# Gated sigmoid (GLU): the loads from tile 2 on issued by GpSimd's software DMA queue

## The chip, the cores and the metric

One Trainium2 chip, one of its cores. The metric is device time in microseconds (us), the median over runs of the whole kernel. The core has five engines that matter here by these names: DVE (VectorE), ACT (ScalarE), POOL (GpSimd), PE (TensorE, not used) and SP (SyncE, which only issues DMAs). Each engine runs its own queue of instructions in order; engines wait for each other by semaphores. A DMA is issued by an engine's queue and carried out by 16 DMA engines, which move data between HBM (main memory) and SBUF (on-chip memory of 128 partitions).

## The reference

```python
def setup_inputs():
    return {
        "x": np.random.randn(8192, 8192).astype(np.float32),
    }

def reference(x: np.ndarray) -> np.ndarray:
    a, b = np.split(x, 2, axis=-1)
    return a * (1 / (1 + np.exp(-b)))
```

The left half of each row is multiplied by the sigmoid of the right half. 268.4 MB are read and 134.2 MB are written, all fp32.

## The kernel before

The 8192 rows are cut into 32 tiles of 256 rows. A tile puts two neighbouring rows of x on each of the 128 partitions (`R = 2`), so each partition's part of a load is one run of 64 KB in HBM and in SBUF, and of a store one run of 32 KB. A tile's load is 8.39 MB, its store 4.19 MB. There are two input buffers (`xs`, called x_sb in the profile) and two output buffers (`os`, called o_sb); tile i uses number i % 2 of each (`SLOTS = 2`).

The loop over tiles (lines 93 to 103) does three things for tile i:

- `work` (line 72): ACT computes the sigmoid of the right half in place (line 82), then a multiply writes the output buffer (line 84). A middle tile is worked in two pieces: columns 0 to 768 of both halves' 4096 (`cut`, the shape 128x1536 with two rows to a partition), whose multiply runs on POOL from tile 2 on, and the rest (128x6656), whose multiply runs on DVE. Tile 0 and tile 31 are worked in four pieces of 128x2048, with all multiplies on DVE.
- `load(i + 2)` (line 59): the load into the input buffer that tile i has just been read from. It waits for the multiplies of tile i, on POOL and on DVE. It is issued on SP's queue (line 63). Loads 0 and 1 are issued ahead of the loop, load 0 in two halves.
- `store(i)` (line 66): issued on ACT's queue (line 68) after the multiplies of tile i. Tile 0 stores in halves as its pieces are done, tile 31 in a half and two quarters.

In the middle tiles, ACT's sigmoid waits for the tile's load and also for the store of tile i - 2, which frees the output buffer (line 81); the multiplies then need no wait of their own for it.

The order on each queue is the program's order (`place`, line 48), and waits that follow from others are dropped there. `_launch_early` (line 106) puts the first load, on SP, ahead of the entry's barrier. `_close_on_sync` (line 119) rewrites the end: POOL waits for all semaphores but the last store's and clears them, and SP waits for the last store.

Of the kernel before, what the change touches and what calls it, by code (L numbers as in the profile page):

```python
# [8 lines left out]
def _tiles(ctx, tc, x, out):  # L9
    nc = tc.nc  # L10
    P = nc.NUM_PARTITIONS
    DEP = mybir.DependencyInfo(mybir.DependencyClass.Sync, mybir.DependencyReason.DATA)
    fp32 = mybir.dt.float32
    SIG = mybir.ActivationFunctionType.Sigmoid

    n_rows, n_cols = x.shape
    half = n_cols // 2
    R = 2
    SLOTS = 2
    n_tiles = n_rows // (P * R)  # L20
    x_g = x.rearrange("(g p h r) m -> g h p (r m)", p=P, h=2, r=R)
    out_g = out.rearrange("(g p h r) m -> g h p (r m)", p=P, h=2, r=R)

    pool = ctx.enter_context(tc.tile_pool(name="io", bufs=1))
    xs = [pool.tile([P, R * n_cols], fp32, name=f"x_sb{k}") for k in range(SLOTS)]
    os = [pool.tile([P, R * half], fp32, name=f"o_sb{k}") for k in range(SLOTS)]

    whole = [(0, 8)]
    rows = [(0, 4), (4, 8)]
    cut = half // 16 * 3  # L30
    few_and_most = [(0, 8, 0, cut), (0, 8, cut, half)]
    fourths = [(k, k + 2, k % 4 * half // 4, (k % 4 + 2) * half // 4) for k in range(0, 8, 2)]
    loads = [whole] * n_tiles
    works = [few_and_most] * n_tiles
    stores = [whole] * n_tiles
    behind = [0] * n_tiles
    loads[0] = stores[0] = rows
    works[0] = works[-1] = fourths
    stores[-1] = [(0, 4), (4, 6), (6, 8)]
    behind[-1] = 1  # L40

    def meet(a, b):
        return a[0] < b[1] and b[0] < a[1]

    traced = [[] for _ in range(SLOTS)]
    load_of, mul_of, store_of = {}, {}, {}

    def place(i, ins, *needs):


        kept = {n.ins.name for n in needs}
        for e in traced[i % SLOTS]:
            if e.ins.name not in kept:
                tc.declare_no_dep(ins.ins, e.ins, reason="follows from the waits that are kept")
        traced[i % SLOTS].append(ins)
        tc.keep_in_program_order(ins)
        return ins

    def load(i):
        for lo, hi in loads[i]:  # L60
            c = slice(lo * n_cols // 4, hi * n_cols // 4)
            free = [m for w, m in mul_of.get(i - SLOTS, []) if meet(w, (lo, hi))]
            ins = nc.sync.dma_start(out=xs[i % SLOTS][:, c], in_=x_g[i // 2, i % 2, :, c])  # L63
            load_of.setdefault(i, []).append(((lo, hi), place(i, ins, *free)))

    def store(i, lo, hi):
        c = slice(lo * half // 4, hi * half // 4)
        ins = nc.scalar.dma_start(out=out_g[i // 2, i % 2, :, c], in_=os[i % SLOTS][:, c])  # L68
        done = [m for w, m in mul_of[i] if meet(w, (lo, hi))]
        store_of.setdefault(i, []).append(((lo, hi), place(i, ins, *done)))  # L70

    def work(i, lo, hi, near, far):

        rows = xs[i % SLOTS].rearrange("p (r h m) -> p r h m", r=R, h=2)
        packed = os[i % SLOTS].rearrange("p (r m) -> p r m", r=R)
        r, c = slice(lo // 4, (hi + 3) // 4), slice(near, far)
        b = rows[:, r, 1, c]
        landed = [s for w, s in load_of[i] if meet(w, (lo, hi))]
        gone = [s for w, s in store_of.get(i - SLOTS, []) if meet(w, (lo, hi))]
        by_sigmoid = 0 < i < n_tiles - 1  # L80
        needs = [*landed, *(gone if by_sigmoid else ())]
        sig = place(i, nc.scalar.activation(out=b, in_=b, func=SIG), *needs)  # L82
        engine = nc.gpsimd if far == cut and i > 1 else nc.vector
        mul = engine.tensor_mul(out=packed[:, r, c], in0=rows[:, r, 0, c], in1=b)  # L84
        if by_sigmoid:
            for s in gone:
                tc.add_manual_dep(sig.ins, s.ins.name, DEP, reason="frees the output slot")
        place(i, mul, sig, *(() if by_sigmoid else gone))
        mul_of.setdefault(i, []).append(((lo, hi), mul))

    for i in range(SLOTS):
        load(i)
    for i in range(n_tiles):
        due = list(stores[i])
        for k, piece in enumerate(works[i]):
            work(i, *piece)
            ready = works[i][k - behind[i]][1] if k >= behind[i] else 0
            while len(stores[i]) > 1 and k < len(works[i]) - 1 and due[0][1] <= ready:
                store(i, *due.pop(0))
        if i + SLOTS < n_tiles:  # L100
            load(i + SLOTS)
        for lo, hi in due:
            store(i, lo, hi)
# [115 lines left out]
```

## Time and profile before

| | |
|---|---|
| Median of 3 runs | 932.47 us (932.45 to 932.73) |
| The profiled execution's own time | 932.5 us |
| Its span, first to last instruction | 931.1 us |
| DVE busy, idle before its instructions | 232.5 us, 690.2 us, all for ACT |
| ACT busy, longest wait | 229.8 us, 630.0 us in 29 waits for stores |
| POOL busy, idle | 99.9 us, 787.7 us, for ACT |
| Loads on SP's queue (q1) | 33 DMAs, 4,752 packets, 268.44 MB |
| Stores on ACT's queue (q10) | 35 DMAs, 5,040 packets, 134.22 MB |
| Issue to landing, median | load 43.5 us, store 43.6 us |

How to read the profile: the span is cut into 40 equal slices, and one digit gives the busy share of a slice in tenths (9 is 90% or more); DMA is the mean over the 16 DMA engines. A queue row gives packets, MB and the share of 16 engines' span that its packets took. A timeline row gives the start and the length in us, the engine and line, the operation with out<-in, the count, and in brackets how long the engine sat idle before and for whom; "SPq" and "ACTq" are issues of DMAs, and where several instructions are merged in a row its length runs from the first to the last of them. The chain is the work that ended last, followed back from the end of the span. A row of the stretch table gives the stretch, its length, the busy time and the number of instructions of DVE, ACT and POOL, the TensorE clock, the DMA share and the GB/s moved. Small packets of under 512 B are those that end a DMA, 16 to each.

### The profile page before, as it was taken

The numbers are of one execution on the slowest core, as the hardware profiler recorded it, in microseconds if no ns is written. First come the engines' busy times: TensorE is split into PE (matmuls) and PEld (weight loads), VectorE is DVE, ScalarE is ACT, GpSimd is POOL, SyncE is SP. The second block draws the span as 40 slices with busy tenths as digits, with TensorE's granted clock in tenths as the row PEclk, the third lists the DMA queues.
The fourth block names the chain that finished last, engine by engine and source line by source line (L and its number), as shares of the span: only waits on it lengthen the run. The fifth ranks groups of instructions, "written<-read, shape, count | busy, mean of one in ns | idle before, by whom it ended". The sixth has DMA issues, their size and how long they took to land.

```text
span 931.1 us, 325 instructions
## 1 busy us (share of the span) xinstructions
DVE 232.5 (25%) x39; ACT 229.8 (25%) x69; POOL 99.9 (11%) x33
## 2 busy tenths in 40 slices
DVE  1133311333113331133320333203332033320233
ACT  2123332033320333203332023320233302333023
POOL 0001111011110111101111011110111101111010
DMA  9999999999999999999999999999999999999998
GB/s 405 450 439 417 428 450 424 455 405 428 450 428 450 407 469 409 428 450 427 452 405 450 428 428 450 424 452 408 428 450 428 450 408 465 411 428 450 427 452 383
DMA packets 9793, 402.67 MB, mean 432 GB/s; under 512 B 1088, under 2 KB 1088, under 8 KB 1088
## 3 DMA queue, kind: packets, MB, share of 16 engines
q1 hardware_dynamic: 4752, 268.44, 66.6%
q10 hardware_dynamic: 5040, 134.22, 33.4%
q14 instruction: 1, 0.01, 0.0%
HBM read 268.44 MB, written 134.22 MB: 432 GB/s over the span
## 4 chain that ended last, share of the span: by engine, by line
DMA 75%; DVE 12%; ACT 12%; issue 0%; ACTq 0%; SPq 0%
DMA out_dram<-o_sb 65%; DVE o_sb L84 12%; ACT x_sb L82 12%; DMA x_sb<-in_x_dram 10%; ACTq L68 0%; SPq L63 0%
## 5 line engine op out<-in xcount | busy, mean ns | idle before, releaser
L84 DVE TENSOR_TENSOR o_sb<-x_sb 128x6656 f32<-128x6656 f32 (+2 forms) x39 | 232.5, 5970 | 690.2 <-ACT x_sb L82 690.2
L82 ACT ACTIVATE x_sb<-x_sb 128x1536 f32<-128x1536 f32 (+1 forms) x68 | 228.5, 3407 | 689.9 <-DMA out_dram<-o_sb 630.0
L84 POOL TENSOR_TENSOR o_sb<-x_sb 128x1536 f32<-128x1536 f32 x29 | 99.7, 3437 | 787.7 <-ACT x_sb L82 787.7
L82 ACT ACT_TABLE_LOAD x1 | 1.3, 1283 | 0.8 <-PEq L203 0.8
L203 POOL MEMSET const-float32-0.0<- 128x1 f32 x1 | 0.1, 98 | 0.2 <-issue 0.2
L203 POOL MEMSET const-bfloat16-1.0<- 128x1 bf16 x1 | 0.1, 101 | 0.0
L203 POOL MEMSET const-uint8-127<- 128x1 uint8 x1 | 0.1, 101 | 0.0
L203 POOL MEMSET const-float32-1.0<- 128x1 f32 x1 | 0.1, 98 | 0.0
## 6 DMA issues: line engine op xcount, KB each, us to landing
out_dram<-o_sb ACTq DMA_DIRECT2D x30, 4096.0 KB, 43.6
x_sb<-in_x_dram SPq DMA_DIRECT2D x2, 4096.0 KB, 16.4
out_dram<-o_sb ACTq DMA_DIRECT2D x3, 2048.0 KB, 28.0
out_dram<-o_sb ACTq DMA_DIRECT2D x2, 1024.0 KB, 8.3
x_sb<-in_x_dram SPq DMA_DIRECT2D x31, 43.5
```

What stands on the lines that cost most here:

```text
L82: sig = place(i, nc.scalar.activation(out=b, in_=b, func=SIG), *needs)
L84: mul = engine.tensor_mul(out=packed[:, r, c], in0=rows[:, r, 0, c], in1=b)
L203: nc = _bacc.Bacc("TRN2", target_bir_lowering=False, num_devices=1)
```

## The change

From tile 2 on, a load is issued by GpSimd instead of SP. Loads 0 (two halves) and 1 stay on SP. The buffers, the bytes, the access patterns, what a load waits for and the place of its issue in the program stay as they are, and the stores stay on ACT's queue.

```diff
@@ -60,7 +60,8 @@
         for lo, hi in loads[i]:
             c = slice(lo * n_cols // 4, hi * n_cols // 4)
             free = [m for w, m in mul_of.get(i - SLOTS, []) if meet(w, (lo, hi))]
-            ins = nc.sync.dma_start(out=xs[i % SLOTS][:, c], in_=x_g[i // 2, i % 2, :, c])
+            queue = nc.sync if i < SLOTS else nc.gpsimd
+            ins = queue.dma_start(out=xs[i % SLOTS][:, c], in_=x_g[i // 2, i % 2, :, c])
             load_of.setdefault(i, []).append(((lo, hi), place(i, ins, *free)))
```

## The prediction

> **What bounds the kernel now.** I read the page's summary, its queues and its chain first, then the DMA view and the timeline of two tiles in the middle, then the stretch table of the end.
>
> ```profile
> span 931.1 us, 325 instructions
> DVE 232.5 (25%) x39; ACT 229.8 (25%) x69; POOL 99.9 (11%) x33
> DMA  9999999999999999999999999999999999999998
> q1 hardware_dynamic: 4752, 268.44, 66.6%
> q10 hardware_dynamic: 5040, 134.22, 33.4%
> DMA 75%; DVE 12%; ACT 12%; issue 0%; ACTq 0%; SPq 0%
> x_sb<-in_x_dram SPq DMA_DIRECT2D x31, 43.5
> ```
>
> Every compute engine idles for three quarters of the span, and the DMA engines never do. The chain names DVE and ACT for 24%, but the row of DMA shares is 9 right through: while they work, the transfers of other tiles go on. So the time is bytes over rate, 402.67 MB at 432 GB/s.
>
> One stretch of two tiles, 506 to 564 us, in the DMA view and the stretch table:
>
> ```profile
> DMA packets 576, 25.17 MB, mean 434 GB/s; under 512 B 64, under 2 KB 64, under 8 KB 64
> q1 hardware_dynamic: 288, 16.78, 66.7%
> q10 hardware_dynamic: 288, 8.39, 33.5%
> 506.00:564.00 58.00, 14.18 (x2) 14.28 (x5) 6.87 (x2) 1.00 1.00 434
> ```
>
> 288 packets for two loads is 2 x (128 rows + 16 small ones); a row of a load is one packet of 64 KB, a row of a store one of 32 KB. A load packet takes 0.667 x 16 x 58 / 256 = 2.418 us of its engine, a store packet 0.335 x 16 x 58 / 256 = 1.214 us. Eight of each per tile and engine are 19.3 + 9.7 = 29.0 us, and a tile takes 29.0 us. Twice 1.214 less 2.418 leaves 0.010 us: the fixed cost of a packet.
>
> The timeline from 99 us shows the slack:
>
> ```profile
> 99.66 7.12 ACT L82 ACTIVATE x_sb<-x_sb 128x1536 f32<-128x1536 f32 x2 [21.82 <-DMA out_dram<-o_sb]
> 101.22 3.44 POOL L84 TENSOR_TENSOR o_sb<-x_sb 128x1536 f32<-128x1536 f32 x1 [25.51 <-ACT x_sb L82]
> 106.81 7.09 DVE L84 TENSOR_TENSOR o_sb<-x_sb 128x6656 f32<-128x6656 f32 x1 [21.85 <-ACT x_sb L82]
> 113.97 29.33 SPq L63 DMA_DIRECT2D x_sb<-in_x_dram  x2
> 113.99 0.35 ACTq L68 DMA_DIRECT2D out_dram<-o_sb  x1
> 128.66 7.12 ACT L82 ACTIVATE x_sb<-x_sb 128x1536 f32<-128x1536 f32 x2 [21.88 <-DMA out_dram<-o_sb]
> 130.22 3.44 POOL L84 TENSOR_TENSOR o_sb<-x_sb 128x1536 f32<-128x1536 f32 x1 [25.56 <-ACT x_sb L82]
> ```
>
> A tile is worked in 14.3 us (99.66 to 113.97), and then its x slot's next load and its store are issued together. That load lands 43.5 us later, of which its own packets, one for one with the stores, take 29.0. For the first 14.5 us it only queues behind the load before it.
>
> **The change, part by part.** Thirty of 33 load DMAs (4,320 of the 4,752 packets, 30 x 8.39 = 251.7 MB) leave SP for POOL.
>
> Removed: 30 issues of 0.33 us on SP, which runs nothing else and spends its time waiting. Worth 0.
>
> Moved, issue: the load waits for DVE's multiply at L84, now on POOL. Ahead of it there stands only POOL's own 3.44 us multiply of that tile, ended at 104.7, before DVE's at 113.9. Behind it stands POOL's multiply of the next tile at 130.22, which itself waits for ACT's work on a load that lands later. POOL is free for 130.2 - 114.0 = 16.2 us. Stores stay on ACT's queue and pass nothing. Worth 0.
>
> Added, making the descriptors by software: no row shows it. Below it is SP's 0.33 us; above, POOL's fixed work is seen only inside a 3.44 us multiply. I take the upper row. The cover is the 14.5 us of the load before, so either is hidden; the first one (tile 2, issued after 28 us) has load 1 in the queue until 46.3 us. Past 14.5 us the load is late, ACT's next sigmoid is late with it, and stores fill the engines for a while. Worth 0.
>
> A rule of the Trainium skill speaks against this part: SBUF — State Buffer, "SBUF: two separate sides", says that a GpSimd-issued DMA cannot write its descriptors while VectorE holds the port pair they share. In this trace DVE ends its multiply before the load is released and starts its next one 21.9 us later, so even a full lock would cost nothing; by rule and by row the sum is the same here unless generation lasts those 21.9 us.
>
> Moved, transfer: this is the only part on the path that sets the end. Each engine carries 30 x 8 = 240 of these packets, so each 10 ns more or less on a packet is 2.4 us. Low end: the whole fixed part vanishes, -2.4 us. High end: each 64 KB row is cut into sixteen 4 KB pieces, each paying 10 ns: 15 x 0.010 x 240 = +36 us. The access pattern and the bytes are unchanged, and the nearest row is the same row on the hardware queue, so I take 0 and keep -2.4 and +36.
>
> The end, which depends on the shares of the two queues:
>
> ```profile
> 897.20 0.34 ACTq L68 DMA_DIRECT2D out_dram<-o_sb  x1
> 911.66 5.51 ACT L82 ACTIVATE x_sb<-x_sb 128x2048 f32<-128x2048 f32 x3 [21.67 <-DMA x_sb<-in_x_dram]
> 918.13 0.34 ACTq L68 DMA_DIRECT2D out_dram<-o_sb  x1
> ```
>
> When load 31 lands at 911.7, store 30 (issued 897.2, behind store 29) still has its 9.7 us to go, until 921.4; the last tile's first store is issued at 918.1, so the engines stay full, and 9.7 us more end at 931.1, the span. One load packet for one store packet keeps this. Worth 0.
>
> Sum: span 931.1 + 0 = 931.1. The profiled run took 932.5, 1.4 more than its span, and the median is 932.47; what lies outside the span is kept. Forecast **932.5 us**. About 0.2% (1.9 us) is what a measurement of this kernel can tell from no change.
>
> **Rivals.**
>
> *Dearer or smaller packets (slower).* The software queue cuts rows, or its packets cost the engines more. It decides from 8 ns a packet (240 x 0.008 = 1.9 us). For it: the engines have no idle time to hide any of it. Against: nothing in the access pattern changes. With rows in halves, 32 KB against 32 KB, the fixed part costs 240 x 0.010 = 2.4 us, and stores get half of the engines: in the 14.5 us before load 31 lands, store 30 moves 7.2 of its 9.7 us, 2.5 are left, and the engines stand empty until the first store at 6.5 + 0.3 us: 4.3 us. Time 932.5 + 6.7 = 939. With 4 KB pieces, 36 + 6.8 = 43, time 975. Unequal engines belong here: one engine 1% slower on loads costs 1% of 30 x 19.3, 5.8 us, time 938. A sentence on the skill: DMA: Bandwidth & Descriptors, "Latency and other measured facts", says that engines 7 and 15 usually lag and suspects the software rings; it gives no size, and the present shares, all on hardware queues, cannot show it.
>
> *A load's whole share as one packet (slower).* If a queue is left only after all eight rows of an engine (19.3 us), loads push stores aside, both x slots fill, and ACT waits for the store that frees the output slot (29 times already, 630.0 us in the waits). Then two tiles take 14.3 of work, one store packet (1.2), a load (19.3), one store packet (1.2), a load (19.3) and the other six packets of the store that ACT waits for (7.3): 62.6 us instead of 58.0, because only one store (9.7 us) is there to cover 14.3 us of work. 15 pairs x 4.6 = 69, time 1,002. Against: today's queues change over after each row. The same page of the skill, "Queues, rings and completion order", calls 9 to 17 descriptors per packet typical; its section "SWDGE vs HWDGE vs iDMA" has packets of preferably 4096 B, which would leave a row by itself.
>
> *A late issue (slower).* Generation holds POOL longer than the 14.5 us of cover. At 20 us each slot's cycle of two tiles grows by at most 20 - 14.5 = 5.5 us (less where stores have drained meanwhile and the load runs alone), 15 x 5.5 = 83, time up to 1,015. Against: 44 times SP's issue would be needed.
>
> *Cheaper packets (faster).* The fixed 10 ns falls away on loads: 932.5 - 2.4 = 930.1. More is not to be had, since the bytes already move at 434 GB/s.
>
> That the change does nothing is excluded by its text; it would show as 4,752 packets on q1.
>
> **How the numbers follow.** Forecast 0.43 (931 to 934), dearer or smaller packets 0.30, whole share 0.10, late issue 0.07, cheaper 0.10. The predicted time is the forecast's. The range runs from 929.8 (just below the cheaper packets) to 955, which takes in the halves, the uneven engines and about a third of the way to the 4 KB pieces: 0.43 + 0.10 + some 0.25 + 0.02 is 0.80. Faster 0.10, same 0.43, slower 0.30 + 0.10 + 0.07 = 0.47.
>
> **What would show it.** Right: q1 keeps 432 packets, a new queue has 4,320 with a share near 62.4% (66.6 x 30 / 32); tiles 29.0 us apart; sigmoid starts unmoved against landings; POOL's multiply not later. Dearer packets: more of them or a larger share for the same bytes. Whole share: tiles in pairs, DMA slices below 9. Late issue: loads begin long after DVE ends. I am wrong if steady tiles move by over 0.06 us each, or the gap after the last load grows beyond 19.5 us.

## The result, and the profile after

The changed kernel takes 940.59 us (median of 4 runs, 940.3 to 940.8) against 932.5: a ratio of 1.0085, 95% interval 1.0073 to 1.0097. It is slower by 8.1 us, under 1% and well clear of the noise. The time lies inside the range, on the slower side; the forecast itself, no change, was wrong.

From the page of the changed kernel, its span, queues and chain, and the row of the issues on POOL:

```profile
span 939.4 us, 329 instructions
DMA  9998999999999999999999999999999999999998
q0 software_dynamic: 4320, 251.66, 61.9%
q10 hardware_dynamic: 5040, 134.22, 33.2%
q1 hardware_dynamic: 432, 16.78, 4.2%
DMA 70%; issue 12%; ACT 10%; DVE 4%; another core or an unknown queue 3%; ACTq 0%; POOLq 0%
L64 POOL DMA_DIRECT2D x_sb<-in_x_dram x30 | 17.8, 594 | 346.3 <-issue 215.7
```

The new queue q0 has the 4,320 packets that were to move, and they are no dearer: 0.619 (the 61.9%) x 16 x 939.4 us over 3,840 rows of data is 2.42 us, as before. An issue keeps POOL for 0.594 us. The only digit that differs in kind is the 8 in the fourth slice, 70 to 94 us. The middle is unchanged too; the stretch 506 to 564 us in the DMA view:

```profile
DMA packets 576, 25.17 MB, mean 434 GB/s; under 512 B 64, under 2 KB 64, under 8 KB 64
q0 software_dynamic: 288, 16.78, 66.7%
q10 hardware_dynamic: 288, 8.39, 33.5%
```

This is row for row what the kernel before has there, with q0 in the place of q1. The loss is at both ends. Rows of the timeline of the start, in the kernel before and then in the changed kernel:

```profile
46.29 7.12 ACT L82 ACTIVATE x_sb<-x_sb 128x1536 f32<-128x1536 f32 x2 [20.90 <-DMA x_sb<-in_x_dram]
70.71 7.12 ACT L82 ACTIVATE x_sb<-x_sb 128x1536 f32<-128x1536 f32 x2 [17.30 <-DMA out_dram<-o_sb]
```

```profile
28.44 0.71 POOL L64 DMA_DIRECT2D x_sb<-in_x_dram  x1 [28.00 <-DVE o_sb L85]
58.41 7.12 ACT L83 ACTIVATE x_sb<-x_sb 128x1536 f32<-128x1536 f32 x2 [33.01 <-DMA x_sb<-in_x_dram]
72.97 0.53 POOL L64 DMA_DIRECT2D x_sb<-in_x_dram  x1 [43.81 <-DVE o_sb L85]
73.16 7.12 ACT L83 ACTIVATE x_sb<-x_sb 128x1536 f32<-128x1536 f32 x2 [7.62 <-DVE o_sb L85]
108.50 7.12 ACT L83 ACTIVATE x_sb<-x_sb 128x1536 f32<-128x1536 f32 x2 [28.22 <-DMA x_sb<-in_x_dram]
```

Tile 1 starts at 58.41 us; it started at 46.29. Tile 2 starts at 73.16, straight after tile 1: its load was there already. The DMA view says why, first of the kernel before while it waits for load 1 (28.4 to 46.3 us), then of the changed kernel (28.5 to 58.4):

```profile
q1 hardware_dynamic: 112, 6.29, 81.2%
q10 hardware_dynamic: 112, 1.57, 20.5%
```

```profile
q0 software_dynamic: 96, 6.29, 48.7%
q1 hardware_dynamic: 96, 5.24, 41.2%
q10 hardware_dynamic: 112, 1.57, 12.3%
```

In the changed kernel load 1 (q1), load 2 (q0) and store 0 (q10) share the engines packet by packet: without the 16 small ones that end a DMA, the three queues have 80, 96 and 96 packets. On one queue load 2 stands behind load 1; on a queue of its own it stands beside it. By 58.4 us load 2 has 6.29 of its 8.39 MB, and load 1 is 12 us late. What follows, in the stretch table of the changed kernel (stretch, its length, busy time of DVE, ACT and POOL, TensorE clock, DMA share, GB/s):

```profile
28.40:58.40 30.00, 0.00 (x0) 0.00 (x0) 0.71 (x1) 1.00 1.02 437
69.50:73.50 4.00, 3.16 (x1) 0.34 (x1) 0.53 (x1) 1.00 0.10 41
926.00:929.00 3.00, 3.00 (x2) 1.66 (x2) 0.00 (x0) 1.00 0.16 66
```

While three queues share, the rate is full (437 GB/s), so the sharing itself loses nothing. But when load 1 lands, both input buffers are nearly full and little is left to move, the rest of load 2 and of store 0 (2.1 MB each). The next transfers are issued 14.3 us (a store) and 14.6 us (a load) later, when tile 1 has been worked, and the engines run dry: a share of 0.10 over 4 us, 3.6 us lost. The second hole is at the end, 3 us at 0.16, 2.5 us lost. The waits name its cause, before and after, and so do the stores' times from issue to landing, before and after:

```profile
ACT x_sb L82 <- DMA out_dram<-o_sb: 630.0, 29, 22.1
ACT x_sb L83 <- DMA x_sb<-in_x_dram: 690.8, 32, 33.0
out_dram<-o_sb ACTq DMA_DIRECT2D x30, 4096.0 KB, 43.6
out_dram<-o_sb ACTq DMA_DIRECT2D x30, 4096.0 KB, 32.7
```

Before, ACT waited 630.0 us in 29 waits for stores; now in 32 waits it is loads. A store used to land 43.6 us after its issue and now lands after 32.7. So the stores' arrears, by which they had been landing late since the first tiles, are gone: during the wait for load 1 and the dry stretch, stores caught up. So after load 31 lands, at 921.6, less is left of store 30 than the 9.7 us of before, and the engines empty before the last tile's first store at 928.08:

```profile
921.61 5.51 ACT L83 ACTIVATE x_sb<-x_sb 128x2048 f32<-128x2048 f32 x3 [21.81 <-DMA x_sb<-in_x_dram]
928.08 0.34 ACTq L69 DMA_DIRECT2D out_dram<-o_sb  x1
```

3.6 and 2.5 are 6.1 of the 8.1 us. The trace's record of each packet accounts for the other 2: packets that ran longer than they do in the middle (2.418 us for a row of a load, 1.213 for a row of a store) add up, per DMA engine, to 2.3 us more than before, 1.2 of it in loads and 1.1 in stores; most of it, 1.6, stands between 75 and 110 us, just after the first dry stretch. What made these packets longer was not found. In the middle the tiles' starts drift by 0.9 us in 26 tiles (tile 4 to tile 30, 755.07 against 754.20 us), 0.03 a tile. The account is complete without this, and packets that match it were not found.

### The profile page after: what moved, and what is told of

It reads as the page before. It is cut to its first block, busy times and chain, and to the rows that moved or that the text cites. A ratio compares the mean times of both kernels' runs of the same rounds, so it can differ in the third digit from the quotient of the medians.

```text
span 939.4 us, 329 instructions
## 1 busy us (share of the span) xinstructions
DVE 232.5 (25%) x39; ACT 229.8 (24%) x69; POOL 117.6 (13%) x63
## 3 DMA queue, kind: packets, MB, share of 16 engines
q0 software_dynamic: 4320, 251.66, 61.9%
## 4 chain that ended last, share of the span: by engine, by line
DMA 70%; issue 12%; ACT 10%; DVE 4%; another core or an unknown queue 3%; ACTq 0%; POOLq 0%
DMA x_sb<-in_x_dram 70%; ACT x_sb L83 10%; DVE o_sb L85 4%; ACTq L69 0%; POOLq L64 0%
## 5 line engine op out<-in xcount | busy, mean ns | idle before, releaser
L64 POOL DMA_DIRECT2D x_sb<-in_x_dram x30 | 17.8, 594 | 346.3 <-issue 215.7
## 6 DMA issues: line engine op xcount, KB each, us to landing
out_dram<-o_sb ACTq DMA_DIRECT2D x30, 4096.0 KB, 32.7
```

The lines of the kernel that those rows point to most:

```text
L64: ins = queue.dma_start(out=xs[i % SLOTS][:, c], in_=x_g[i // 2, i % 2, :, c])
```

## The experiments

The theory, called "handover" in the expectations: nothing about the software queue costs time; it is that two neighbouring loads stand on two queues, once, at a moment when one store is all the other work there is. The rivals: a one-off cost when the software queue is first used, and dearer packets on it. Landings and packets that stand in no row shown here are from the traces' records of each packet. Each kernel was timed beside the kernel before on the same chip, and ratios are to it.

**Keeping the two loads apart.**

```diff
+            if i == SLOTS:
+                for _, s in load_of[i - 1]:
+                    tc.add_manual_dep(ins.ins, s.ins.name, DEP, reason="the load before has landed")
```

> Load 2, the first on POOL, also waits until load 1 has landed. Handover (two loads on two queues share the engines, so load 1 lands 12 us late, the engines run dry near 70 us and the backlog of stores is spent): load 1 lands at 46.3 us again, no dry stretch but for the 1 to 2 us that load 2 takes to start, which the rest of store 0 (1.2 MB, 2.7 us) fills; time 932.5 to 934.5. One-off start of the software queue, or dearer packets on it: the same software packets in the same number, so 940.6.

Measured: 936.40 us, ratio 1.0038 (1.0025 to 1.0051). The same software packets, 4.2 us less than the changed kernel: neither rival allows that. But it is 1.9 us over what the handover theory expected at most. Tile 1 is back in its place and the hole near 70 us is gone; the hole at the end is not. Its timeline and stretch table:

```profile
46.31 7.12 ACT L86 ACTIVATE x_sb<-x_sb 128x1536 f32<-128x1536 f32 x2 [20.93 <-DMA x_sb<-in_x_dram]
76.76 7.12 ACT L86 ACTIVATE x_sb<-x_sb 128x1536 f32<-128x1536 f32 x2 [23.33 <-DMA x_sb<-in_x_dram]
...
921.00:925.00 4.00, 4.00 (x3) 2.66 (x3) 0.00 (x0) 1.00 0.08 33
```

A share of 0.08 over 4 us leaves 3.7 us empty, but a stretch counts each packet by its start. Counted to their ends over the whole span, the engines stand empty 3.0 us longer than in the kernel before, and longer packets add 1.4 us: the 4.4 us by which this execution's span, 935.5 us, is longer. Load 2 was issued at 46.91, and its first packet started at 50.37, 3.5 us later where 1 to 2 had been expected; meanwhile store 0 moved alone and finished at 50.79 (the expectation counted that as filling), and from then on no store was in arrears (33.8 us from issue to landing): tile 2 starts at 76.76, 6 us late, with its input the last thing to come. The expectation missed that work done early by stores is work missing at the end. The start itself is no price of the software queue: load 2 in the changed kernel has its first packet 4.9 us after its issue, and on ACT's hardware queue, in the first kernel of the handover between two hardware queues below, 4.8 us.

**The same change, one tile later and in the middle.**

```diff
-            queue = nc.sync if i < SLOTS else nc.gpsimd
+            queue = nc.sync if i < 3 else nc.gpsimd
```

> The loads change queue one tile later, at tile 3. Handover: load 3 is issued when load 2 is the older one and store 1 has just been queued; sharing 2 to 2 to 1, load 2 lands some 6 us late, but load 3 and store 1 then have about 12.6 + 6.4 = 19 us of work left, more than the 14.3 us of a tile's work, so nothing runs dry: 932.5 to 934. One-off start of the software queue: 940.6. Dearer packets: 29 of 30 loads still software, 940.3.

> The loads change queue at tile 16. Handover: load 15 lands some 10 us late, but 9.7 us of load 16 and 9.7 us of store 14 are left, 19 us against 14.3, so no dry stretch: sigmoids from tile 15 on start about 10 us late, the store backlog at the end is that much smaller, and the time is 932.5 to 933.5. One-off start: 940.6. Dearer packets: half of the loads, 936.5.

Measured: from tile 3, 933.08 us, ratio 1.0004 (0.9996 to 1.0013); from tile 16, 932.73 us, ratio 1.0014 (1.0002 to 1.0026). Both times are where the handover theory put them, and neither rival is left: with the change at tile 3, 29 of the 30 software loads and the first use of the queue cost nothing that can be told from no change. At tile 16, nine of the 12 executions took 932.6 to 933.6 us and three took 936.6 to 938.3; the trace is of one of the nine, so what the three lost stays open. The sharing does take place. With the change at tile 16, tile 15 starts 36 us after tile 14 instead of 29 and tile 16 follows after 26.5, yet no engine is short of work:

```profile
419.00:455.00 36.00, 7.09 (x1) 7.12 (x2) 4.16 (x2) 1.00 1.01 437
455.00:470.00 15.00, 7.09 (x1) 7.12 (x2) 3.44 (x1) 1.00 0.97 419
470.00:482.00 12.00, 0.00 (x0) 0.18 (x1) 0.59 (x1) 1.00 1.01 437
```

The stretch in which tile 15 is worked, 455 to 470, is the one that ran dry when the change was at tile 2. Here it has a share of 0.97, because a half load and a whole store were left. The details of the second expectation were missed: it had tiles from 15 on some 10 us late and the arrears of stores smaller at the end. Tile 15 was 7.4 us late and the tiles after it about 5, and the arrears were larger: load 31 started tile 31 at 910.33 instead of 911.66, with store 29 still on its way. While two loads share with one store, loads gain on stores (9.43 MB against 3.15 from 426.4 to 455.3 us). The waits of the kernel from tile 3 show the arrears there too, as before:

```profile
ACT x_sb L83 <- DMA out_dram<-o_sb: 635.3, 29, 22.3
```

**The handover between two hardware queues.** Here no load is software: loads 0 and 1 on SP, the others on ACT, and the stores of tiles 0 to 30 on POOL, so that a third queue carries them. Beside it, the same with all loads on SP.

```diff
-            queue = nc.sync if i < SLOTS else nc.gpsimd
+            queue = nc.sync if i < SLOTS else nc.scalar
...
-        ins = nc.scalar.dma_start(out=out_g[i // 2, i % 2, :, c], in_=os[i % SLOTS][:, c])
+        queue = nc.gpsimd if i < n_tiles - 1 else nc.scalar
+        ins = queue.dma_start(out=out_g[i // 2, i % 2, :, c], in_=os[i % SLOTS][:, c])
```

> No load is software any more: loads 0 and 1 on SP, loads 2 to 31 on ACT's hardware queue; the stores of tiles 0 to 30 go to POOL's software queue, those of tile 31 stay on ACT. Handover: load 1 and load 2 overlap on two hardware queues as they do on SP and POOL; load 1 lands near 58 us, the engines run dry for about 3 us near 70 us, and the time is 6 to 9 us above the next kernel. A price of software loads (one-off or by the packet): none of it is left, so the same as the next kernel within 1 us.

> The same with all loads on SP: stores of tiles 0 to 30 on POOL's software queue. Handover: no two load queues overlap, so near before, 932.5 to 935. Dearer software packets: half the bytes of the changed kernel go through software, about 936.

Measured: with the handover 957.38 us, ratio 1.0265 (1.0251 to 1.0279); on one queue 933.25, ratio 1.0006 (0.9997 to 1.0015). So the hole needs no software load. The timeline and stretch table of the first:

```profile
58.80 7.12 ACT L84 ACTIVATE x_sb<-x_sb 128x1536 f32<-128x1536 f32 x2 [33.33 <-DMA x_sb<-in_x_dram]
...
70.00:73.50 3.50, 3.05 (x1) 0.00 (x0) 0.16 (x1) 1.00 0.00 0
```

Tile 1 starts at 58.80, and for 3.5 us nothing moves at all: the same first hole as in the changed kernel. The second hole is absent. Here the stores fall behind again after the first one (44.5 us from issue to landing), and the engines stay full from load 31 to the last tile's first store; why the arrears came back here and not in the changed kernel was not found. The size was missed, 24 us over the kernel on one queue instead of 6 to 9. Nearly all of the rest, 19 us per engine, is load packets that ran longer than 2.418 us, spread over the middle, where tiles are 29.6 us apart:

```profile
158.00:506.00 348.00, 84.05 (x12) 85.47 (x24) 47.72 (x23) 1.00 1.00 426
```

The engines are busy there (share 1.00) and slower (426 GB/s). Two readings were put to a test: that loads on ACT's queue beside software stores cost it, or that it came with the disturbed start. The edit is `i < 3` in place of `i < SLOTS` in the first line above.

> The kernel with loads on SP then ACT and stores on POOL, but with the change of load queue at tile 3 instead of 2. Handover: the dry stretch of 3.95 us near 70 us goes and the store backlog stays. Its other 17 us (tiles 29.6 us apart instead of 29.0) have two readings. If loads on ACT's queue beside software stores cost it, tiles stay 29.6 apart and the time is 948 to 952; if it came with the disturbed start, tiles are 29.0 apart and the time is 932.5 to 934.5.

Measured: 932.94 us, ratio 1.0004 (0.9995 to 1.0013), tiles 29.0 us apart. With the change of queue one tile later both the hole and the slow middle are gone, so the pair of queues is not slow by itself; that the disturbed start causes the slow middle is the reading that is left, and not shown beyond that. What kept the packets long for 27 tiles after a disturbed start was not found.

**One software queue from the first load.** All loads on POOL; there is then no load on SP to launch early, so the control has all loads on SP without the early launch.

```diff
-            queue = nc.sync if i < SLOTS else nc.gpsimd
+            queue = nc.gpsimd
...
-    _launch_early(nc)
```

> All loads on POOL, 0 and 1 too; the early launch of the first load on SP is left out, since it has no load there. Handover: one queue for all loads, no dry stretch later; only the start is later, 1 to 2 us, so within 2 us of the next kernel. Dearer packets or a one-off start of the software queue of 8 us: 6 to 10 us above the next kernel.

> All loads on SP without the early launch, the control of the kernel before it. All theories: before plus what the early launch saves, 933 to 935.

Measured: 934.84 us, ratio 1.0026 (1.0016 to 1.0037), and 933.36, ratio 1.0007 (0.9998 to 1.0016). The medians differ by 1.5 us, inside the 2 us of the expectation. At the start, where nothing hides it, the first sigmoid begins at 13.94 us against 12.64; of these 1.3 us, 0.5 is that POOL comes to its first issue later than SP (1.26 against 0.74 us). The trace is of an execution of 936.96 us, 2.1 above the median, and it shows engines partly idle at the end too (a share of 0.73 over 922 to 926 us); whether the other executions have that, no trace shows.

**The hole at the end.** The last tile is stored in four quarters, in the changed kernel and in the kernel before.

```diff
-    stores[-1] = [(0, 4), (4, 6), (6, 8)]
+    stores[-1] = [(0, 2), (2, 4), (4, 6), (6, 8)]
```

> The changed kernel with the last tile stored in four quarters instead of a half and two quarters, so that its first store is issued 4.3 us after load 31 has landed, not 6.5. Handover, whose second half is that the store backlog is spent and the engines run dry for 2.7 us before that first store: about 2 us of it go, 938 to 939. If the dry stretch at the end costs nothing or has another cause: 940.6.

> The same edit in the kernel before. Handover: store 30 still covers the engines for 9.7 us after load 31 has landed, so an earlier first store moves nothing: 932.3 to 932.8. Rival (an earlier first store is worth 2 us anywhere): 930.5.

Measured: the changed kernel 938.57 us (2.0 less), ratio to the kernel before 1.0064 (1.0051 to 1.0076); the kernel before with the edit 932.70, ratio 1.0001 (0.9992 to 1.0010). An earlier first store is worth 2 us where the engines stand empty and nothing where they don't. The stretch table of the changed kernel with the edit, where a share of 0.16 stood:

```profile
926.00:929.00 3.00, 2.84 (x2) 2.71 (x2) 0.00 (x0) 1.00 0.94 388
```

No version beats the kernel before. With its engines full from the first load to the last store, the order of transfers can lose time there but hardly win any.

## Why the prediction was right and wrong

*What bounds the kernel* was right: bytes over rate. Every kernel above that keeps the engines fed is within 0.15% of before but for the all-software one (0.26%), and the changed kernel's loss is mostly time without a transfer.

*Removed and moved issues, descriptors by software*, each worth 0: right as far as cost goes. POOL's issue is 0.594 us, between the bounds of 0.33 and 3.44, and POOL's next multiply is not held up.

*The port rule* of the Trainium skill (SBUF — State Buffer, "SBUF: two separate sides") showed no effect: the issues take 0.53 to 0.71 us, at times when DVE idles. No run here shows what it would do beside a busy DVE.

*Moved, transfer*, worth 0 with ends of -2.4 and +36: right at 0. A row of a load is one packet of 2.418 us on either queue, in 98% of the 3,840 rows of q0. That rejects dearer, smaller and cheaper packets and uneven engines; the 96 and 80 packets side by side reject the whole share as one packet, and the issues 0.3 to 0.6 us after DVE's multiply ends reject the late issue. The rivals' prices of 938 and 939 lie near the measured time, but that is chance: their causes are absent. So it is luck, too, that the range holds the time: its slower side was there for these rivals. (Its end, 955, is about half of the way to the 975 of 4 KB pieces, not a third.) The Trainium skill, DMA: Bandwidth & Descriptors, says in "Queues, rings and completion order" that 9 to 17 descriptors a packet are typical; the 4,320 packets here are 30 x (128 rows + 16), a packet to a row.

*The step that failed* is the cover of the first issue: "the first one (tile 2, issued after 28 us) has load 1 in the queue until 46.3 us". That sentence lets the new queue stand behind the old one. Load 1 is on SP's queue and load 2 on POOL's, so load 2 takes turns with load 1 from its first packet on (33.4 us), and load 1 landed at 58.4. This cost the first hole, 3.6 us. The share of packets was worked out for loads against stores and never for loads against loads. No rival named it.

*The end*, "One load packet for one store packet keeps this. Worth 0.", failed for the same reason. The share was kept, but what covers the end is not the share: it is the arrears of stores, which the disturbed start used up: 2.5 us. The mechanism was in the text, in the rival that had store 30 done too early and the engines empty until the last tile's first store; it came from another cause.

Two signs that the forecast had set for itself held: the gap after the last load was to stay under 19.5 us, and steady tiles were not to move by over 0.06. Both are so (17.8, and 0.03), and the time still moved: the gap after the last load shrank while what came before grew by 10. The signs looked at the middle and the end; the change of queue, the one event in the kernel, was not among them.

## What to carry to other kernels

A queue is also an order: moving some transfers of a stream to another queue ends the order between the last one left and the first one moved, and with packets shared evenly the older, the one that work is waiting for, lands late. Whether that costs anything depends on how much other transfer work is outstanding at that moment; count it against the compute time until the next issue (here 14.3 us), and change queues where it is larger. In this kernel one tile later was enough. In a kernel that is bound by its transfers, look also at what is in arrears: stores that are late all along cost nothing and cover the end, and whatever lets them catch up is paid for there.

## What the runs showed of the hardware that was not expected

After a disturbed start, loads on ACT's queue and software stores on POOL's ran at 426 GB/s with busy engines for 27 tiles, 29.6 us a tile; the same queues ran 29.0 us a tile when they were joined one tile later. Load packets of up to 3.5 us instead of 2.418 stand from about 1 us before each tile's first sigmoid to 6 us after it. The cause is open.
